# Layer 1's residual: scaled and shifted on VectorE in layer 0, loaded in pieces behind the weights

## The chip, the cores and the metric

The kernel runs on one core of one Trainium2 chip. The metric is the device time of one execution in microseconds (us). A core has TensorE (PE: matmuls and transposes), VectorE (DVE), ScalarE (ACT), GpSimd (POOL) and SyncE (SP, which here only issues loads and stores). Each engine runs its instructions in the order in which they were put, and waits on semaphores for the others.

## What is computed

Two layers of a decoder trunk on 256 tokens of width 2048, in fp32. Layer 0 is a gated linear recurrence (HGRN2), layer 1 a sparse attention (NSA). Each ends alike, with an out projection and a layer norm of the sum with its own input:

```python
def _layer_norm(x, g, b):
    mu = jnp.mean(x, -1, keepdims=True)
    xc = x - mu
    var = jnp.mean(xc * xc, -1, keepdims=True)
    return xc * lax.rsqrt(var + LN_EPS) * g + b

h = x
for i in range(2):
    y = _hgrn2_mixer(h, ...) if i == 0 else _nsa_mixer(h, ...)   # both end in (gate * o) @ w_out
    h = _layer_norm(DEEPNORM_ALPHA * h + y, ln_g[i], ln_b[i])
```

So layer 0's normed output h is needed twice in layer 1: as the input of its projections, transposed, and at the end of the layer as the residual, token by token.

## The kernel before

**Tiles.** Tokens are two tiles `t` of 128 (NT = 2). A weights tile is 256 rows by 512 columns, 512 KB: SyncE loads it as `wr` (`load`, L105), ScalarE rounds it to `wh`, and VectorE computes `wl` = `wr` - `wh` (`split`, L78 and L79), with AHEAD as their priority. A product is three matmuls: high times high, high times low, low times high (L140 to L142 in `tok_step`). A tile of weights is thus twelve matmuls of 512 columns for both token tiles. Activations are pairs of the same kind: `ah`, `al` for layer inputs (`hT.put`), `bh`, `bl` for what goes into an out projection. There are 3 slots for `wr`, 5 for `wh` and 5 for `wl`, with 1, 3 and 3 more while the pool "wide" is open (`widen`, `slot`).

**Out projection of layer 0** (L504 to L533). Four groups of 512 columns, `c` = 0 to 3, eight weights tiles each. For c < 3 both token tiles go together (`project`), and `residual` adds alpha times `xr`, a piece of x that GpSimd's queue loads (L508), into `hb` and takes statistics (L511, L512). For c = 3 the token tiles go one after the other (`project_by_tile`): `finish(t)` takes the last residual, mean and variance (L496, L497, then a power on GpSimd, L224), normalises `hb` in place (L519, four pieces), has TensorE transpose it (L196, sixteen), ScalarE scale and shift it by the norm's gain and bias (L524), which are per partition there, and splits it into `ah` and `al`. Then `hb`, normalised but neither scaled nor shifted, is stored to DRAM as `norm0` (L527, GpSimd's queue), token tile by token tile.

**Seam to layer 1.** The first projection of layer 1 (the keys, KC) runs by token tile as well. `issue_after` puts its steps for tile 0 from the eighth on (HOLD = 7) behind the last transposes of layer 0; the first seven may run ahead of them. The last transpose is what `finish` returns.

**Layer 1's out projection** (L827 on). The same four groups. `fetch(c)`, called behind the fourth weights tile, loads a piece of `norm0` (`xr`) and pieces of layer 0's gain and bias into `gb`, on SyncE's queue (L808, L811; `gb` has one buffer), and GpSimd scales and shifts `xr` (L813, L814), two passes for each token tile. `residual` adds it to the projection into `hb` (L837) and takes statistics (L839). `row` loads layer 1's own gain and bias, 1 MB each (L819), after group 1, where `widen` opens the extra slots too.

**What sets the order.** The tile framework schedules every engine from a simulated timeline and priorities. The pieces of the engines' orders further down show what came out of it for the changed places.

Of the kernel before, what the change touches and what calls it, by code (L numbers as in the profile page):

```python
# [8 lines left out]
F32 = mybir.dt.float32  # L9
# [3 lines left out]
OP = mybir.AluOpType  # L13
# [4 lines left out]
D = 2048  # L18
S = 256
NT = S // 128  # L20
KT = D // 128
KG = KT // 4
DEPTH = 2
ALPHA = (2 * DEPTH) ** 0.25
# [30 lines left out]
def trunk(ctx, tc, a, out):  # L55
    nc = tc.nc
    pe, act, dve, pool = nc.tensor, nc.scalar, nc.vector, nc.gpsimd
# [7 lines left out]
    pj = ctx.enter_context(tc.tile_pool(name="pj", bufs=4, space=PSUM))  # L65
    mx = ctx.enter_context(tc.tile_pool(name="mx", bufs=4, space=PSUM))
    dram = ctx.enter_context(tc.tile_pool(name="dram", bufs=1, space=DRAM))
    norm0 = dram.tile([S, D], F32, name="norm0")

    def pjb(shape):  # L70
        return pj.tile(shape, F32, name="pjb", tag="pjb")
# [127 lines left out]
    last = [None]  # L199
# [113 lines left out]
    with tc.tile_pool(name="start", bufs=4) as start:  # L313
# [3 lines left out]
        ps = mxb([128, 128])  # L317
# [182 lines left out]

    hT = Pair("a")
    with tc.tile_pool(name="n0", bufs=2) as n0:
        hb = n0.tile([128, NT, D], F32, name="hb", bufs=1)
        stats = n0.tile([128, NT, 4, 6], F32, name="stats", bufs=1)  # L504
        for c in range(4):
            cs = slice(512 * c, 512 * (c + 1))
            xr = n0.tile([128, NT, 512], F32, name="xr")
            nc.gpsimd.dma_start(xr, x[:, cs].rearrange("(t p) d -> p t d", p=128))  # L508

            def residual(t, ps, c=c, cs=cs, xr=xr):  # L510
                dve.scalar_tensor_tensor(hb[:, t, cs], xr[:, t], ALPHA, ps, op0=OP.mult, op1=OP.add)  # L511
                dve.bn_stats(stats[:, t, c], hb[:, t, cs])  # L512

            def finish(t, ps):
                residual(t, ps)
                mv = moments(n0, hb, stats, t)
                for g in range(KG):
                    h = hb[:, t, 512 * g:512 * (g + 1)]
                    dve.tensor_scalar(h, h, mv[:, 0:1], mv[:, 3:4], op0=OP.subtract, op1=OP.mult)  # L519
                    ps = transposed(h.rearrange("p (k d) -> p k d", d=128))  # L520
                    h1 = n0.tile([128, 4, 128], F32, name="h1")
                    for k in range(4):
                        n = 4 * g + k
                        act.activation(h1[:, k], ps[:, k], AF.Identity, scale=g0c[:, n:n + 1],  # L524
                                       bias=b0c[:, n:n + 1])
                    hT.put(g, t, h1)
                nc.gpsimd.dma_start(norm0[128 * t:128 * (t + 1), :], hb[:, t])  # L527
                return last[0]

            if c < 3:  # L530
                for t, ps in enumerate(project(oT, a["l0_w_out"], 512 * c)):
                    residual(t, ps)
            else:  # L533
                normed = project_by_tile(oT, a["l0_w_out"], 512 * c, finish)
# [96 lines left out]
    with tc.tile_pool(name="cmp", bufs=1) as cp:  # L631
# [29 lines left out]
        h = ck.hidden()  # L661
        ps = mxb([128, 4, NB])
# [8 lines left out]
        h = cv.hidden()  # L671
# [5 lines left out]
        ps = mxb([128, 4, 128])  # L677
# [4 lines left out]
        ps = ps.rearrange("p g d -> p (g d)")  # L682
# [9 lines left out]
        n = (512 + 48) // 2  # L692
# [109 lines left out]
    stats = n1.tile([128, NT, 8, 6], F32, name="stats", bufs=1)  # L802


    def fetch(c):
        cs = slice(512 * c, 512 * (c + 1))
        xr = n1.tile([128, NT, 512], F32, name="xr")
        nc.sync.dma_start(xr, norm0[:, cs].rearrange("(t p) d -> p t d", p=128))  # L808
        gb = n1.tile([128, 2, 512], F32, name="gb", bufs=1)
        for i, name in enumerate(("l0_ln_g", "l0_ln_b")):  # L810
            nc.sync.dma_start(gb[:, i], a[name][None, cs].to_broadcast([128, 512]))  # L811
        for t in range(NT):
            pool.tensor_tensor(xr[:, t], xr[:, t], gb[:, 0], op=OP.mult)  # L813
            pool.tensor_tensor(xr[:, t], xr[:, t], gb[:, 1], op=OP.add)  # L814
        return xr

    def row(name):
        r = n1.tile([128, D], F32, name=name, bufs=1)
        nc.sync.dma_start(r, a[name][None, :].to_broadcast([128, D]))  # L819
        return r  # L820


    for c in range(4):
        cs = slice(512 * c, 512 * (c + 1))

        xr = []

        def behind(j, c=c, xr=xr):
            if j == 3:
                xr.append(fetch(c))  # L830

        def residual(t, ps, c=c, xr=xr, parts=range(2)):
            xr = xr[0]
            n = ps.shape[1] // len(parts)
            for i, u in enumerate(parts):
                h = hb[:, t, 512 * c + 256 * u:512 * c + 256 * (u + 1)]
                dve.scalar_tensor_tensor(h, xr[:, t, 256 * u:256 * (u + 1)], ALPHA, ps[:, n * i:n * (i + 1)],  # L837
                                         op0=OP.mult, op1=OP.add)
                dve.bn_stats(stats[:, t, 2 * c + u], h)  # L839

        def finish(t, ps):
# [20 lines left out]
        if c < 3:  # L862
            for t, ps in enumerate(project(oT, a["l1_w_out"], 512 * c, behind)):
                residual(t, ps)
            if c == 2:
                last_xr = fetch(3)
            if c == 1:
                widen()
                g1, b1 = row("l1_ln_g"), row("l1_ln_b")
        else:  # L870
            xr.append(last_xr)
            project_by_tile(oT, a["l1_w_out"], 512 * c, finish, halve=True)
    wide.close()

# [32 lines left out]
```

## Time and profile before

| | us |
|---|---|
| median of three runs | 1019.64 |
| the runs | 1019.52, 1019.64, 1021.37 |
| the profiled execution | 1021.53 |
| its span | 1019.8 |
| TensorE busy | 999.9 (98%) |
| VectorE busy | 669.6 (66%) |
| ScalarE busy | 543.3 (53%) |
| GpSimd busy | 143.1 (14%) |
| mean granted clock of TensorE | 0.994 |

The profile is of one execution. Its rows give start and duration in us from the span's start, the engine, the line, output and input tile, and in brackets the idle time of that engine just before, with what ended it. Matmuls of 512 columns show durations of 0.39 to 0.40 but overlap: one starts every 0.2335 us, and a distance above that between two starts is time lost. The other engines' instructions overlap at their ends too, so that steps between starts are shorter than durations.

### The profile page before, as it was taken

The numbers are of one execution on the slowest core, as the hardware profiler recorded it, in microseconds if no ns is written. First come the engines' busy times: TensorE is split into PE (matmuls) and PEld (weight loads), VectorE is DVE, ScalarE is ACT, GpSimd is POOL, SyncE is SP. The second block draws the span as 40 slices with busy tenths as digits, with TensorE's granted clock in tenths as the row PEclk, the third lists the DMA queues.
The fourth block names the chain that finished last, engine by engine and source line by source line (L and its number), as shares of the span: only waits on it lengthen the run. The fifth ranks groups of instructions, "written<-read, shape, count | busy, mean of one in ns | idle before, by whom it ended". The sixth has DMA issues, their size and how long they took to land.

```text
span 1019.8 us, 15942 instructions
## 1 busy us (share of the span) xinstructions
PE 999.9 (98%) x6041; PEld 883.4 (87%) x6041; DVE 669.6 (66%) x1095; ACT 543.3 (53%) x864; POOL 143.1 (14%) x222
## 2 busy tenths in 40 slices
PE   9999999999999999999999989999999999999995
PEld 8988998899889988878889878898989889998775
DVE  6796568656866586656565655555857668675566
ACT  6654455445544554434475554454856667775241
POOL 0400300030003000210015410101010022000543
PEclk9999999999999999999999999999999999999998
DMA  8865565555555655557465677577354454345872
GB/s 299 258 218 165 155 184 168 166 155 179 173 166 155 177 176 163 161 180 250 160 208 159 200 226 238 154 222 207 106 166 143 145 165 133 119 144 184 316 240 83
DMA packets 100780, 185.25 MB, mean 182 GB/s; under 512 B 6096, under 2 KB 20512, under 8 KB 100192
## 3 DMA queue, kind: packets, MB, share of 16 engines
q1 hardware_dynamic: 99232, 178.67, 56.7%
q0 software_dynamic: 1472, 5.56, 1.7%
q8 instruction: 47, 0.77, 0.3%
q14 instruction: 29, 0.24, 0.1%
HBM read 180.02 MB, written 4.19 MB: 181 GB/s over the span
## 4 chain that ended last, share of the span: by engine, by line
PE 84%; DMA 7%; DVE 3%; POOL 2%; ACT 2%; issue 1%; SPq 0%; ACTq 0%; DVEq 0%; POOLq 0%
PE pjb L141 15%; PE pjb L142 15%; PE pjb L140 15%; PE pjb L185 10%; PE pjb L187 10%; PE pjb L188 10%; DMA wr<-in_l_w_in_dram 3%; PE mxb L423 2%; DVE wl L79 2%; DMA wr<-in_l_w_out_dram 2%; ACT wh L78 1%; DMA gb<-in_l_ln_g_dram 1%; PE mxb L196 1%; POOL fl L590 1%; PE mxb L546 1%; PE mxb L548 1%
## 5 line engine op out<-in xcount | busy, mean ns | idle before, releaser
L79 DVE TENSOR_TENSOR wl<-wr,wh 128x1024 fp32r<-128x1024 f32 (+2 forms) x330 | 398.9, 1213 | 224.2 <-ACT wh L78 221.5
L78 ACT ACTIVATE wh<-wr 128x1024 fp32r<-128x1024 f32 (+2 forms) x330 | 340.7, 1036 | 346.1 <-PE pjb L142 149.9
L185 PE MATMUL pjb<-ah,wh 128*128 128x256 f32 x832 | 235.8, 284 | 0.5 <-ACT wh L78 0.5
L187 PE MATMUL pjb<-al,wh 128*128 128x256 f32 x832 | 235.9, 284 | 0.0
L188 PE MATMUL pjb<-ah,wl 128*128 128x256 f32 x832 | 234.4, 284 | 0.5 <-DVE wl L79 0.5
L141 PE MATMUL pjb<-wl,ah 128*128 128x512 f32 (+1 forms) x576 | 223.6, 388 | 2.2 <-DVE wl L79 2.1
L142 PE MATMUL pjb<-wh,al 128*128 128x512 f32 (+1 forms) x576 | 222.7, 387 | 0.0
L140 PE MATMUL pjb<-wh,ah 128*128 128x512 f32 (+1 forms) x576 | 221.4, 387 | 1.1 <-ACT wh L78 1.1
L185 PEld LDWEIGHTS pjb<-ah,wh 128*128 128x128 f32 x832 | 157.3, 189 | 1.5 <-ACT wh L78 1.0
L188 PEld LDWEIGHTS pjb<-ah,wl 128*128 128x128 f32 x832 | 156.6, 189 | 1.1 <-DVE wl L79 0.9
L187 PEld LDWEIGHTS pjb<-al,wh 128*128 128x128 f32 x832 | 156.5, 188 | 0.5
L141 PEld LDWEIGHTS pjb<-wl,ah 128*128 128x128 f32 x576 | 108.8, 189 | 26.0 <-DVE wl L79 4.4
L140 PEld LDWEIGHTS pjb<-wh,ah 128*128 128x128 f32 x576 | 108.5, 189 | 23.6 <-ACT wh L78 1.8
L142 PEld LDWEIGHTS pjb<-wh,al 128*128 128x128 f32 x576 | 108.9, 189 | 22.2
L141 PE MATMUL pjb<-wl,bh 128*128 128x512 f32 (+1 forms) x272 | 105.0, 386 | 1.4 <-DVE wl L79 1.3
L142 PE MATMUL pjb<-wh,bl 128*128 128x512 f32 (+1 forms) x272 | 104.1, 384 | 0.0
L140 PE MATMUL pjb<-wh,bh 128*128 128x512 f32 (+1 forms) x272 | 103.1, 384 | 0.8 <-ACT wh L78 0.8
L141 PEld LDWEIGHTS pjb<-wl,bh 128*128 128x128 f32 x272 | 51.2, 188 | 13.9 <-DVE wl L79 3.2
L140 PEld LDWEIGHTS pjb<-wh,bh 128*128 128x128 f32 x272 | 51.1, 188 | 12.3 <-ACT wh L78 1.7
L142 PEld LDWEIGHTS pjb<-wh,bl 128*128 128x128 f32 x272 | 51.3, 189 | 10.4
L486 POOL TENSOR_TENSOR gz<-gz,gn 128x512 f32<-128x512 f32 x8 | 13.5, 1691 | 317.0 <-ACT gz L485 316.4
L557 POOL TENSOR_TENSOR rot<-qr,cc 128x128 f32<-128x128 f32 x14 | 9.5, 678 | 254.1 <-ACT qr L553 253.8
(220 smaller groups left out, 1034.0 us busy)
## 6 DMA issues: line engine op xcount, KB each, us to landing
wr<-in_l_w_in_dram SPq DMA_DIRECT2D x230, 512.0 KB, 3.7
wr<-in_l_w_out_dram SPq DMA_DIRECT2D x64, 512.0 KB, 4.4
wr<-in_l_w_in_dram SPq DMA_DIRECT2D x16, 280.0 KB, 3.0
wr<-in_l_cmp_w_k_dram SPq DMA_DIRECT2D x8, 512.0 KB, 4.4
wr<-in_l_cmp_w_v_dram SPq DMA_DIRECT2D x8, 512.0 KB, 4.3
xr<-in_x_dram POOLq DMA_DIRECT2D x4, 512.0 KB, 5.7
norm<-hb POOLq DMA_DIRECT2D x2, 1024.0 KB, 5.4
xr<-norm SPq DMA_DIRECT2D x4, 512.0 KB, 7.2
```

What stands on the lines that cost most here:

```text
L78: act.activation(hi, src, AF.Copy)
L79: dve.tensor_tensor(lo, src, hi.bitcast(F32), op=OP.subtract)
L140: pe.matmul(ps, xh, wh, start=(k == 0), stop=False)
L141: pe.matmul(ps, xh, wl, start=False, stop=False)
L142: pe.matmul(ps, xl, wh, start=False, stop=(k == KT - 1))
L185: pe.matmul(o, hi[:, kk, c], xh, start=(k == 0 and b % 2 == 0), stop=False, skip_group_check=True)
L187: pe.matmul(o, hi[:, kk, c], xl, start=False, stop=False, skip_group_check=True)
L188: pe.matmul(o, lo[:, kk, c], xh, start=False, stop=(k == KT - 1), skip_group_check=True)
L196: last[0] = pe.transpose(ps[:, i], src[:, i], ident).ins
L423: pe.matmul(ps[:, h], km[:, h].rearrange("p b r j -> p (b r j)"), later, start=True, stop=True)
L486: pool.tensor_tensor(z, z, gn, op=OP.mult)
L546: pe.matmul(o, a[0], b[0], start=start, stop=False)
```

## The change

Layer 0's gain and bias are loaded whole, as rows repeated over 128 partitions, by two loads of 1 MB on GpSimd's queue ahead of layer 0's residual. After the transposes of each token tile, VectorE multiplies and adds them into `hb` in place (16 passes of 128x512 in all), and the result is stored as `res1`. In layer 1 the passes on GpSimd and `fetch` are gone: `res1` is loaded into `hb` itself in four pieces, layer 1's gain and bias in eight pieces, and each call of `behind` puts one of these twelve loads behind a weights tile. `widen` is called after group 0.

```diff
+        rows = []
+        for name in ("l0_ln_g", "l0_ln_b"):
+            r = n0.tile([128, D], F32, name=name, bufs=1)
+            nc.gpsimd.dma_start(r, a[name][None, :].to_broadcast([128, D]))
+            rows.append(r)
         hb = n0.tile([128, NT, D], F32, name="hb", bufs=1)
...
                     hT.put(g, t, h1)
-                nc.gpsimd.dma_start(norm0[128 * t:128 * (t + 1), :], hb[:, t])
-                return last[0]
+                done = last[0]
+                for g in range(KG):
+                    cs = slice(512 * g, 512 * (g + 1))
+                    for r, op in zip(rows, (OP.mult, OP.add)):
+                        dve.tensor_tensor(hb[:, t, cs], hb[:, t, cs], r[:, cs], op=op)
+                nc.gpsimd.dma_start(res1[128 * t:128 * (t + 1), :], hb[:, t])
+                return done
...
-    def fetch(c):
-        cs = slice(512 * c, 512 * (c + 1))
-        xr = n1.tile([128, NT, 512], F32, name="xr")
-        nc.sync.dma_start(xr, norm0[:, cs].rearrange("(t p) d -> p t d", p=128))
-        gb = n1.tile([128, 2, 512], F32, name="gb", bufs=1)
-        for i, name in enumerate(("l0_ln_g", "l0_ln_b")):
-            nc.sync.dma_start(gb[:, i], a[name][None, cs].to_broadcast([128, 512]))
-        for t in range(NT):
-            pool.tensor_tensor(xr[:, t], xr[:, t], gb[:, 0], op=OP.mult)
-            pool.tensor_tensor(xr[:, t], xr[:, t], gb[:, 1], op=OP.add)
-        return xr
...
+    g1, b1 = (n1.tile([128, D], F32, name=name, bufs=1) for name in ("l1_ln_g", "l1_ln_b"))
+    loads = []
+    for c in range(4):
+        cs = slice(512 * c, 512 * (c + 1))
+        loads.append((hb[:, :, cs], res1[:, cs].rearrange("(t p) d -> p t d", p=128)))
     for c in range(4):
         cs = slice(512 * c, 512 * (c + 1))
+        for r, name in ((g1, "l1_ln_g"), (b1, "l1_ln_b")):
+            loads.append((r[:, cs], a[name][None, cs].to_broadcast([128, 512])))
+
+    def behind(j):
+        if loads and j > 0:
+            nc.sync.dma_start(*loads.pop(0))
...
-                dve.scalar_tensor_tensor(h, xr[:, t, 256 * u:256 * (u + 1)], ALPHA, ps[:, n * i:n * (i + 1)],
-                                         op0=OP.mult, op1=OP.add)
+                dve.scalar_tensor_tensor(h, h, ALPHA, ps[:, n * i:n * (i + 1)], op0=OP.mult, op1=OP.add)
...
-            if c == 2:
-                last_xr = fetch(3)
-            if c == 1:
+            if c == 0:
                 widen()
-                g1, b1 = row("l1_ln_g"), row("l1_ln_b")
```

VectorE at the seam, before: from the first `wl` behind tile 0's normalising to tile 1's normalising (L519). L511 is tile 1's residual.

```order
L79 TENSOR_TENSOR wl<-wr,wh 128x1024 x2
L79 TENSOR_TENSOR al<-h_4848,ah 128x4x128
L79 TENSOR_TENSOR wl<-wr,wh 128x1024
L79 TENSOR_TENSOR al<-h_4861,ah 128x4x128
L79 TENSOR_TENSOR wl<-wr,wh 128x1024
L511 SCALAR_TENSOR_TENSOR hb<-xr,pjb 128x512
L512 BN_STATS stats<-hb 128x6
L496 BN_AGGR mv<-stats 128x2
L497 TENSOR_SCALAR mv<-mv 128x1
L79 TENSOR_TENSOR wl<-wr,wh 128x1024
L519 TENSOR_SCALAR hb<-hb,mv 128x512 x4
```

After, the same stretch, with one `wl` ahead of its first row. L537 are the new passes on `hb`, and L516 is tile 1's residual:

```order
L537 TENSOR_TENSOR hb<-hb,l_ln_g 128x512
L79 TENSOR_TENSOR wl<-wr,wh 128x1024
L537 TENSOR_TENSOR hb<-hb,l_ln_g 128x512 x3
L537 TENSOR_TENSOR hb<-hb,l_ln_b 128x512
L79 TENSOR_TENSOR al<-h_4852,ah 128x4x128
L537 TENSOR_TENSOR hb<-hb,l_ln_b 128x512
L79 TENSOR_TENSOR wl<-wr,wh 128x1024
L537 TENSOR_TENSOR hb<-hb,l_ln_b 128x512
L79 TENSOR_TENSOR al<-h_4865,ah 128x4x128
L537 TENSOR_TENSOR hb<-hb,l_ln_b 128x512
L79 TENSOR_TENSOR wl<-wr,wh 128x1024 x2
L516 SCALAR_TENSOR_TENSOR hb<-xr,pjb 128x512
```

Between the residual of tile 1 and its normalising (L524) stand now:

```order
L79 TENSOR_TENSOR wl<-wr,wh 128x1024
L79 TENSOR_TENSOR al<-h_4878,ah 128x4x128
L79 TENSOR_TENSOR wl<-wr,wh 128x1024
L79 TENSOR_TENSOR al<-h_4891,ah 128x4x128
L517 BN_STATS stats<-hb 128x6
L496 BN_AGGR mv<-stats 128x2
L497 TENSOR_SCALAR mv<-mv 128x1
L524 TENSOR_SCALAR hb<-hb,mv 128x512 x4
```

Eight passes and one `wl` have come between tile 0's normalising and tile 1's residual, and two `wl` and two `al` between that residual and its statistics. TensorE's order at this place is the same in both kernels.

SyncE at layer 1's out projection, before (L105 are the weights, L808 and L811 the loads of `fetch`, L819 the rows):

```order
L105 DMA wr<-in_l_w_out_dram 128x2x512 x15
L808 DMA xr<-norm_72 128x2x512
L811 DMA gb<-in_l_ln_g_dram 128x512
L811 DMA gb<-in_l_ln_b_dram 128x512
L808 DMA xr<-norm_72 128x2x512
L819 DMA l_ln_g<-in_l_ln_g_dram 128x2048
L819 DMA l_ln_b<-in_l_ln_b_dram 128x2048
L105 DMA wr<-in_l_w_out_dram 128x2x512 x3
L811 DMA gb<-in_l_ln_g_dram 128x512
L811 DMA gb<-in_l_ln_b_dram 128x512
L808 DMA xr<-norm_72 128x2x512
L105 DMA wr<-in_l_w_out_dram 128x2x512 x3
```

After (L829 are the twelve pieces):

```order
L105 DMA wr<-in_l_w_out_dram 128x2x512 x16
L829 DMA hb<-res_72 128x2x512 x4
L829 DMA l_ln_g<-in_l_ln_g_dram 128x512
L829 DMA l_ln_b<-in_l_ln_b_dram 128x512
L829 DMA l_ln_g<-in_l_ln_g_dram 128x512
L829 DMA l_ln_b<-in_l_ln_b_dram 128x512
L829 DMA l_ln_g<-in_l_ln_g_dram 128x512
L829 DMA l_ln_b<-in_l_ln_b_dram 128x512
L829 DMA l_ln_g<-in_l_ln_g_dram 128x512
L829 DMA l_ln_b<-in_l_ln_b_dram 128x512
L105 DMA wr<-in_l_w_out_dram 128x2x512 x16
```

The twelve pieces stand in one block behind the sixteenth weights tile, where before loads of `fetch` and of weights alternate.

ScalarE at the last gate of layer 1, before: `o` is the last head group's output, `zT` its gate, `bh` what goes into the out projection.

```order
L78 ACTIVATE pt_8778<-mxb 128x512
L78 ACTIVATE wh<-wr 128x1024 x2
L774 ACTIVATE o<-mxb 128x512
L786 ACT_TABLE_LOAD
L786 ACTIVATE zT<-pjb 128x512
L78 ACTIVATE bh<-o 128x4x128 x2
```

After:

```order
L78 ACTIVATE pt_8798<-mxb 128x512
L78 ACTIVATE wh<-wr 128x1024 x2
L785 ACTIVATE o<-mxb 128x512
L78 ACTIVATE wh<-wr 128x1024
L797 ACT_TABLE_LOAD
L797 ACTIVATE zT<-pjb 128x512
```

One `wh` of the out projection has moved from behind `bh` to a place between `o` and the table load for the gate.

## Rows read from the trace of the kernel before

**Rows 1.** Page, parts 1, 4, 5: busy time and share; chain that ended last; ScalarE's `wh`.

```profile
PE 999.9 (98%) x6041; PEld 883.4 (87%) x6041; DVE 669.6 (66%) x1095; ACT 543.3 (53%) x864; POOL 143.1 (14%) x222
...
PE 84%; DMA 7%; DVE 3%; POOL 2%; ACT 2%; issue 1%; SPq 0%; ACTq 0%; DVEq 0%; POOLq 0%
...
L78 ACT ACTIVATE wh<-wr 128x1024 fp32r<-128x1024 f32 (+2 forms) x330 | 340.7, 1036 | 346.1 <-PE pjb L142 149.9
```

**Rows 2.** Timeline of VectorE at the seam: start, duration, line, tile, [idle before].

```profile
502.02 2.35 DVE L79 TENSOR_TENSOR wl<-wr,wh 128x1024 fp32r<-128x1024 f32 x2
...
507.51 0.69 DVE L79 TENSOR_TENSOR al<-h,ah 128x512 fp32r<-128x512 f32 x1
...
508.12 1.22 DVE L79 TENSOR_TENSOR wl<-wr,wh 128x1024 fp32r<-128x1024 f32 x1
...
509.55 0.69 DVE L511 SCALAR_TENSOR_TENSOR hb<-xr,pjb 128x512 f32<-128x512 f32 x1 [0.22 <-PE pjb L142]
...
511.30 0.15 DVE L497 TENSOR_SCALAR mv<-mv 128x1 f32<-128x1 f32 x1
...
512.73 1.91 DVE L519 TENSOR_SCALAR hb<-hb,mv 128x512 f32<-128x512 f32 x4
```

**Rows 3.** Timelines of TensorE and ScalarE at the seam.

```profile
514.27 1.91 PE L196 MATMUL mxb<-ident,hb 128*128 128x128 f32 x16
...
527.73 0.58 ACT L553 ACTIVATE qr<-pjb 128x512 f32<-128x512 f32 x1
```

**Rows 4.** Windows: length, busy us of PE, PEld, DVE, ACT, POOL, clock, DMA share, GB/s.

```profile
598.00:599.00 1.00, 0.04 (x1) 0.04 (x1) 0.10 (x2) 0.91 (x1) 0.00 (x0) 1.00 0.42 146
601.00:602.00 1.00, 1.00 (x3) 0.78 (x3) 1.00 (x2) 0.47 (x2) 0.60 (x2) 0.50 0.54 134
600.00:610.00 10.00, 9.78 (x48) 8.32 (x49) 5.84 (x7) 6.26 (x11) 1.54 (x4) 0.83 0.78 245
```

**Rows 5.** Timelines of GpSimd, VectorE and TensorE in layer 0's out projection.

```profile
448.95 1.47 POOL L508 DMA_DIRECT2D xr<-in_x_dram  x2 [6.48 <-PE mxb L231]
...
454.69 1.28 DVE L511 SCALAR_TENSOR_TENSOR hb<-xr,pjb 128x512 f32<-128x512 f32 x2 [1.97 <-DMA xr<-in_x_dram]
...
462.62 0.40 PE L140 MATMUL pjb<-wh,bh 128*128 128x512 f32 x1
```

**Rows 6.** DMA issues: queue, count, size of one, median us from issue to landing.

```profile
xr<-in_x_dram POOLq DMA_DIRECT2D x4, 512.0 KB, 5.7
...
norm<-hb POOLq DMA_DIRECT2D x2, 1024.0 KB, 5.4
...
l_ln_b<-in_l_ln_b_dram SPq DMA_DIRECT2D x1, 1024.0 KB, 11.7
```

**Rows 7.** TensorE in layer 1's out projection: timeline at two places, one window.

```profile
953.39 0.40 PE L142 MATMUL pjb<-wh,bl 128*128 128x512 f32 x1
...
955.55 0.40 PE L142 MATMUL pjb<-wh,bl 128*128 128x512 f32 x1
...
990.50 0.40 PE L140 MATMUL pjb<-wh,bh 128*128 128x512 f32 x1
...
995.19 0.39 PE L142 MATMUL pjb<-wh,bl 128*128 128x512 f32 x1
...
950.00:960.00 10.00, 9.32 (x40) 6.89 (x38) 4.53 (x3) 3.57 (x4) 3.80 (x3) 1.00 1.02 378
```

**Rows 8.** Timelines of SyncE (first `xr`) and TensorE (its last matmul).

```profile
937.31 0.37 SPq L808 DMA_DIRECT2D xr<-norm  x1
...
1008.21 0.28 PE L142 MATMUL pjb<-wh,bl 128*128 128x256 f32 x1
```

**Rows 9.** Timelines of ScalarE and TensorE at the last gate of layer 1.

```profile
932.90 1.28 ACT L786 ACT_TABLE_LOAD   x1
...
934.19 0.60 ACT L786 ACTIVATE zT<-pjb 128x512 f32<-128x512 f32 x1
...
935.35 0.40 PE L140 MATMUL pjb<-wh,bh 128*128 128x512 f32 x1
```

More of the change, by code (lines that the diff above doesn't have):

```diff
@@ L67, in trunk @@
     dram = ctx.enter_context(tc.tile_pool(name="dram", bufs=1, space=DRAM))
-    norm0 = dram.tile([S, D], F32, name="norm0")
+    res1 = dram.tile([S, D], F32, name="res1")
     def pjb(shape):
@@ L802, in trunk, with residual @@
     stats = n1.tile([128, NT, 8, 6], F32, name="stats", bufs=1)
-    def fetch(c):
-        cs = slice(512 * c, 512 * (c + 1))
-        xr = n1.tile([128, NT, 512], F32, name="xr")
-        nc.sync.dma_start(xr, norm0[:, cs].rearrange("(t p) d -> p t d", p=128))
-        gb = n1.tile([128, 2, 512], F32, name="gb", bufs=1)
-        for i, name in enumerate(("l0_ln_g", "l0_ln_b")):
-            nc.sync.dma_start(gb[:, i], a[name][None, cs].to_broadcast([128, 512]))
-        for t in range(NT):
-            pool.tensor_tensor(xr[:, t], xr[:, t], gb[:, 0], op=OP.mult)
-            pool.tensor_tensor(xr[:, t], xr[:, t], gb[:, 1], op=OP.add)
-        return xr
[L817 to L820, printed above, removed]
+    g1, b1 = (n1.tile([128, D], F32, name=name, bufs=1) for name in ("l1_ln_g", "l1_ln_b"))
+    loads = []
     for c in range(4):
         cs = slice(512 * c, 512 * (c + 1))
[L826 to L833, printed above, removed]
+        loads.append((hb[:, :, cs], res1[:, cs].rearrange("(t p) d -> p t d", p=128)))
[6 more added lines that the diff above has]
+            nc.sync.dma_start(*loads.pop(0))
+    for c in range(4):
+        cs = slice(512 * c, 512 * (c + 1))
+        def residual(t, ps, c=c, parts=range(2)):
             n = ps.shape[1] // len(parts)
@@ L864, in trunk @@
                 residual(t, ps)
-            if c == 2:
-                last_xr = fetch(3)
-            if c == 1:
+            if c == 0:
                 widen()
-                g1, b1 = row("l1_ln_g"), row("l1_ln_b")
         else:
-            xr.append(last_xr)
             project_by_tile(oT, a["l1_w_out"], 512 * c, finish, halve=True)
```

## The prediction

> **What bounds the kernel now.** I read the shares first: TensorE is busy 98% of the span and the chain that ended last is 84% TensorE [rows 1]. So a step costs or gives time only where TensorE then waits, and the question for each edit is whether TensorE's own order reaches an instruction before its input is there. Next I read the timelines of VectorE and TensorE at the seam of layer 0 and layer 1 [rows 2, 3], because the change puts new work on VectorE there. Then the table of short windows for what a pause of TensorE does to its clock [rows 4], the start of layer 0's out projection [rows 5, 6], and the out projection of layer 1, where rows and weights share the loads [rows 7, 8, 9]. The span of the profiled execution is 1019.8 us inside a run of 1021.53; the median of the runs is 1019.64. My sum is a difference, made from the profiled rows and added to the median.
>
> **Part 1: sixteen VectorE passes at the seam.** Layer 0's last column group goes token tile by token tile. After tile 0 the changed order holds eight scale or shift passes (L537) between tile 0's normalising and tile 1's residual (the order of VectorE above). In before that stretch runs from 502.02 to 509.55 with four `wl`, two `al` and about 1.5 us of waiting [rows 2]. Two `wl` in a row took 2.35 us, the second of them 1.22 as always, so a `wl` steps by 1.13; an `al` of 128x512 steps by 0.61 (507.51 to 508.12). No row shows an in-place `hb` pass; the nearest is that `al`, also a two-input fp32 pass of 128x512 in SBUF, and the four normalising passes of the same size with one tensor input are a lower bound (from 1.91 us for four). I take 0.61.
>
> The new stretch has five `wl`, two `al` and eight passes: 5 x 1.13 + 10 x 0.61 = 11.75 us, so tile 1's residual starts at 502.02 + 11.75 = 513.8 instead of 509.55. VectorE is in order, so everything behind it is late too. Behind that residual the new order has two `wl` and two `al` ahead of the statistics, which before had one `wl`, beside GpSimd's power: 2 x 1.13 + 2 x 0.61 = 3.5 us. The residual, its statistics and the two small steps are 1.75 us from L511 to L497 [rows 2], and from L497 to a first scaled tile some 0.9 us more (0.25 for L497 and 0.6 for the power on GpSimd). So tile 1's normalising starts at 513.8 + 3.5 + 1.75 + 0.9 = 519.9, where before it started at 512.73. Its first pass takes 0.5, and the transposes can begin at 520.4.
>
> TensorE reached those transposes at 514.27 without waiting [rows 3]. Its order is the same in the changed kernel: all it may do ahead of them is tile 0's first seven steps of the next projection, and these end at 514.27. **It waits 520.4 - 514.27 = 6.1 us.** The bounds are 5.0 (passes at 0.48) and 7.0 (passes at their full 0.69). Tile 1's own eight passes stand behind its normalising, off the path. All later work hangs on TensorE, so nothing absorbs the loss. The stores of the scaled tiles are late too: tile 1's leaves GpSimd's queue behind its passes, at 519.9 + 1.9 + 8 x 0.61 + 2 x 0.61 = 527.9; with the landing of before, 5.4 [rows 3, 6], that is 533.3. The rotary copies that take over the space come at 527.73 [rows 3] behind TensorE's next tile, so with the pause and the clock at 535.5 or later: no cost, 1 us at most if the passes run late.
>
> **The clock after that pause.** In before TensorE was busy for 0.04 of the microsecond from 598; from 601 the granted clock read 0.50 (1.2 GHz), and 0.83 over 600 to 610, with 1.00 before and after [rows 4]. That is 10 x 0.17 = 1.7 us of matmul time lost after a pause of little over 1 us. A pause of 6 us should cost as much: **+1.7**, with 1.0 and 3.3 (twice the row, for a longer pause) as bounds.
>
> **Part 2: two whole rows loaded ahead of layer 0's residual.** Each is 1 MB, on GpSimd's queue, and the first `xr` (0.52 MB) stands behind them. In before that `xr` was issued at 448.95 and the first residual began at 454.69 [rows 5]. TensorE needs that residual's PSUM bank back for the third column group, whose first matmul is at 462.62 [rows 5], by counting back from 514.27. Now 2.62 MB go ahead of it. At the best rate of a row, 378 GB/s [rows 7], that is 6.9 us; the plain `xr` of before took 5.7 to land [rows 6], of which 1.4 is its bytes at this rate, so 4.3 are latency and sharing: 448.95 + 6.9 + 4.3 = 460.2, in time. If the weights keep half the rate, 13.9 + 4.3 gives 467.1, and with 0.7 for the residual TensorE waits 5.2 us. The second whole-row load of layer 1 landed 11.7 us after its issue with 2.5 MB queued ahead of its own [rows 6], some 300 GB/s, nearer to the fast end. I take **+1.0**, bounds 0 and 5.2. The split weights have 5 + 3 slots here, tiles of twelve matmuls, 2.8 us each, so they are ahead by enough to cover a VectorE that stands still for 10 us.
>
> The Trainium skill, page "DMA: Bandwidth & Descriptors", section "Queues, rings and completion order", says that each DMA engine takes turns between the queues that have work, a packet at a time. By that rule the slow end would hold whenever weights are queued, and the sum would be 4 us longer; no row here shows the shares of two busy queues, so it is a rival below.
>
> **Part 3: layer 1's out projection loses its fetches.** In before, eight multiplies and eight adds on GpSimd prepare `xr`; the loads of `gb` wait in SyncE's queue for these, with weights behind them. TensorE pays in two places. From 953.39 to 955.55 it took 2.16 us for four steps of 0.2335, a loss of 1.23. From 990.50 to 995.19 it took 4.69 us for eight such steps and six halves, a loss of 2.1 [rows 7]. Together 3.35 us.
>
> In the changed order SyncE issues sixteen weights tiles, then the twelve pieces, then sixteen weights (the order above). No piece waits for GpSimd, and 4 MB of rows are loaded in place of 6 MB. The wait for the last `bl` at the head of the pieces stays, as `xr` had it. The pieces start where the first `xr` load stood, 937.31; 4.2 million bytes at 378 GB/s take 11 us, and with 4.3 of latency and 1.4 of its own bytes the seventeenth tile lands by 954, split by 957. TensorE ends at 1008.2 [rows 8], and the last sixteen tiles are 45 us of it, or 48 with the loss at 990: it is wanted at about 960. So I expect **-3.35** (bounds -3.35 and 0; the tile is in time by 3 us, so I take the full gain).
>
> **Part 4: the extra slots open one group earlier.** A sixteenth tile is loaded before the pieces, and its `wh` now stands on ScalarE between the last `o` and the table load for `zT` (the order of ScalarE above). In before the table load ran at 932.90 and `zT` at 934.19, ended 934.79 [rows 9]. A `wh` takes 1.04 in the mean [rows 1], and more if its tile lands after 932.9: `zT` ends at 935.8 to 936.9. TensorE needs the bank that `zT` reads for the first matmul of group one's token tile 1, at 935.35 [rows 9]. **It waits 0.5 to 1.5; I take +1.1.** The tail behind TensorE's end keeps its order: 0.
>
> **Sum.** 6.1 + 1.7 + 1.0 - 3.35 + 1.1 = +6.55 us. Against the profiled run that is 1028.1, against the median **1026.2 us**.
>
> **Rivals.**
> - *The passes fall into VectorE's idle time.* VectorE was idle a third of the span [rows 1], and 1.5 us at the seam. If the passes cost TensorE nothing, parts 3 and 4 remain: -3.35 + 1.1 = -2.25, 1017.4, faster. It decides when the delay of tile 1's normalising stays under 1 us: its first result was there at 513.2 and was wanted at 514.27. Against it: 4.8 us of passes and three more `al` or `wl` stand in an in-order queue ahead of it. Chance 0.08.
> - *The pieces don't do what they say.* They are not behind single loads any more but in one block of 4 MB, and the tile after them may be late as before. Then none of the 3.35 us comes back: 1019.64 + 9.9 = 1029.5. For it: from 950 to 960 the DMA engines were full, share 1.02 [rows 7]. Against it: the sixteen tiles in front. Chance 0.12.
> - *The whole rows hold up layer 0's first residual*, the slow end of part 2: 4.2 more, and a clock drop of its own of up to 1.7: 1030.4 to 1032.1. Chance 0.10.
> - *The clock is not lowered at the seam.* 1026.2 - 1.7 = 1024.5. Against it the rows at 601. Chance 0.08.
> - *Half price*: passes at 0.48 us and the last `wl` and `al` where TensorE is not waiting, say 3 us, clock 1.0, rows hidden: 3.0 + 1.0 - 2.25 = +1.75, 1021.4, no change. Chance 0.07.
>
> **How the numbers follow.** The forecast has 0.55. Its own terms reach from 1023 (5.0 + 1.0 + 0 - 3.35 + 0.5 = +3.15) to some 1029 with two of them half way to their upper bounds. Leaving out the first rival and half of the slow ends, the range is 1021.3 to 1030. 0.2% is 2 us, about what a measurement of this kernel can tell from no change. Faster: the first rival, 0.08. Same: half price and some of the low end, 0.09. Slower: the rest, 0.83.
>
> **What would show it.** Right: in VectorE's timeline eight passes between tile 0's normalising and tile 1's residual, and tile 1's normalising at about 520; a pause of 5 to 7 us on TensorE in front of the second sixteen transposes, waiting for VectorE; a granted clock of 0.50 for some microseconds behind it; no pauses at 950 to 995 (shifted by 7 to 9 us), and one of about 1 us at the first group for tile 1, waiting for ScalarE's `zT`. Wrong: a pause under 3 us at the seam, or weights that land late behind the pieces; a pause near 463 that waits for VectorE's first residual would mean the slow end of part 2.

## The result and the profile after

The changed kernel takes 1026.04 us in the median of four runs (1024.85 to 1026.49) against 1020.3 of before beside it; the ratio is 1.0051 with an interval of 1.0036 to 1.0066. It is slower by some 5.7 us, where 1026.2 was forecast. The profiled execution of after took 1025.88 (span 1024.2).

The page of after, busy time and the chain, answers to [rows 1]:

```profile
PE 998.6 (98%) x6041; PEld 883.4 (86%) x6041; DVE 677.1 (66%) x1111; ACT 543.2 (53%) x864; POOL 120.9 (12%) x208
...
PE 86%; DMA 5%; DVE 4%; ACT 2%; POOL 1%; issue 1%; SPq 0%; ACTq 0%; DVEq 0%; POOLq 0%
```

TensorE is busy for 1.3 us less than before and the span is 4.4 longer, so it waits 5.7 us more. The list of what TensorE waited for, the three lines that before doesn't have (us in total, times, longest):

```profile
PE mxb L196 <- DVE hb L524: 5.8, 1, 5.8
...
PE pjb L140 <- DVE hb L516: 0.6, 1, 0.6
...
PE pjb L140 <- ACT zT L797: 0.6, 1, 0.6
```

By far the longest is the one of 5.8 us: the transposes wait for the normalising of tile 1. VectorE's timeline at the seam, against [rows 2], and TensorE's, against [rows 3]:

```profile
505.64 1.89 DVE L537 TENSOR_TENSOR hb<-hb,l_ln_g 128x512 f32<-128x512 f32 x3
...
514.46 0.69 DVE L516 SCALAR_TENSOR_TENSOR hb<-xr,pjb 128x512 f32<-128x512 f32 x1
...
520.41 1.92 DVE L524 TENSOR_SCALAR hb<-hb,mv 128x512 f32<-128x512 f32 x4 [0.70 <-POOL mv L224]
```

```profile
514.77 0.40 PE L142 MATMUL pjb<-wh,al 128*128 128x512 f32 x1
...
521.01 3.44 PE L196 MATMUL mxb<-ident,hb 128*128 128x128 f32 x16 [5.84 <-DVE hb L524]
...
524.20 0.48 PE L140 MATMUL pjb<-wh,ah 128*128 128x512 f32 x1
```

In before the next matmul behind the sixteen transposes of 514.27 was this one:

```profile
515.94 0.48 PE L140 MATMUL pjb<-wh,ah 128*128 128x512 f32 x1
```

The passes L537 stand between tile 0 and the residual of tile 1, which starts at 514.46 (509.55 in before); the normalising follows at 520.41 (512.73). TensorE's last matmul ahead of the transposes starts at 514.77 and takes its step of 0.2335, so the transposes are 521.01 - 515.00 = 6.0 us late. From the end of tile 0's normalising to the start of tile 1's, VectorE took 17.65 us against 10.71 in before. The eight passes are 4.8 of the difference, and two `wl` and two `al` that came forward in the order are 3.5; some 1.5 us in which VectorE had been idle took up the rest. Behind the wait the sixteen transposes need 3.19 us to the next matmul, against 1.67 in before (514.27 to 515.94). The windows there (columns as in [rows 4]) show why:

```profile
518.00:520.00 2.00, 0.00 (x0) 0.00 (x0) 1.64 (x5) 0.00 (x0) 0.20 (x1) 0.50 1.05 407
...
522.00:524.00 2.00, 2.00 (x11) 2.00 (x10) 1.97 (x4) 1.84 (x6) 0.00 (x0) 0.50 0.03 8
...
524.00:526.00 2.00, 2.00 (x12) 1.68 (x11) 2.00 (x5) 2.00 (x6) 0.00 (x0) 0.98 0.00 0
```

The granted clock falls in the pause itself, is 0.50 to 524, and 0.98 in the window after that: 3.19 - 1.67 = 1.5 us.

The first residual of layer 0, timelines of GpSimd, VectorE and TensorE, against [rows 5]:

```profile
448.80 0.56 POOL L506 DMA_DIRECT2D l_ln_g<-in_l_ln_g_dram  x1 [6.46 <-PE mxb L231]
...
462.51 1.29 DVE L516 SCALAR_TENSOR_TENSOR hb<-xr,pjb 128x512 f32<-128x512 f32 x2 [3.13 <-DMA xr<-in_x_dram]
...
462.25 0.40 PE L142 MATMUL pjb<-wh,bl 128*128 128x512 f32 x1
...
463.25 0.50 PE L140 MATMUL pjb<-wh,bh 128*128 128x512 f32 x1 [0.60 <-DVE hb L516]
```

`xr` is there at 462.5 and not at 454.7; TensorE loses 1.00 - 0.2335 = 0.77 before the third column group and 0.1 behind it. Layer 1, timelines of SyncE, ScalarE and TensorE, against [rows 7 to 9]:

```profile
946.58 1.90 SPq L829 DMA_DIRECT2D hb<-res  x4
...
956.19 12.22 SPq L105 DMA_DIRECT2D wr<-in_l_w_out_dram  x6
...
941.09 1.06 ACT L78 ACTIVATE wh<-wr 128x1024 fp32r<-128x1024 f32 x1 [0.19 <-DMA wr<-in_l_w_out_dram]
...
942.16 1.28 ACT L797 ACT_TABLE_LOAD   x1
...
943.46 0.60 ACT L797 ACTIVATE zT<-pjb 128x512 f32<-128x512 f32 x1
...
964.27 1.06 ACT L78 ACTIVATE wh<-wr 128x1024 fp32r<-128x1024 f32 x1 [14.59 <-DMA wr<-in_l_w_out_dram]
...
943.14 0.39 PE L142 MATMUL pjb<-wh,bl 128*128 128x512 f32 x1
...
944.11 0.50 PE L140 MATMUL pjb<-wh,bh 128*128 128x512 f32 x1 [0.58 <-ACT zT L797]
```

The pieces stand in a block from 946.58, the next weights tile is issued at 956.19, and its `wh` runs at 964.27. No matmul of TensorE waits for it: from 950 to the end of the projection there is no step with a loss over 0.15, where before has six, 3.3 us in all, and 3.9 with the 0.1 that most of them leave in the step or two behind. The `wh` at 941.09 stands ahead of the table load, and `zT` is 1.2 us late against its place in before; TensorE loses 0.74 and 0.1.

### The profile page after: what moved, and what is told of

Its sections match the earlier page's. It is cut to its first block, busy times and chain, and to the rows that moved or that the text cites. A ratio compares the mean times of both kernels' runs of the same rounds, so it can differ in the third digit from the quotient of the medians.

```text
span 1024.2 us, 15939 instructions
## 1 busy us (share of the span) xinstructions
PE 998.6 (98%) x6041; PEld 883.4 (86%) x6041; DVE 677.1 (66%) x1111; ACT 543.2 (53%) x864; POOL 120.9 (12%) x208
## 4 chain that ended last, share of the span: by engine, by line
PE 86%; DMA 5%; DVE 4%; ACT 2%; POOL 1%; issue 1%; SPq 0%; ACTq 0%; DVEq 0%; POOLq 0%
PE pjb L140 16%; PE pjb L142 15%; PE pjb L141 15%; PE pjb L187 10%; PE pjb L188 10%; PE pjb L185 10%; DMA wr<-in_l_w_in_dram 3%; DVE wl L79 2%; PE mxb L423 2%; ACT wh L78 1%; PE mxb L196 1%; DMA xr<-in_x_dram 1%; POOL fl L601 1%; PE mxb L557 1%; PE mxb L559 1%; PE mxb L558 1%
```

## The experiments

Their ratios are against runs of the kernel before on the same chip (its medians there: 1020.76, 1020.99 and 1020.55). Waits are read as losses: the distance between the starts of two matmuls, less TensorE's step (0.2335 us for 512 columns, half of it for 256). Line numbers shift by a few between the kernels; the tiles' names don't.

**Parts 3 and 4 alone.**

```diff
-        rows = []
-        for name in ("l0_ln_g", "l0_ln_b"):
-            r = n0.tile([128, D], F32, name=name, bufs=1)
-            nc.gpsimd.dma_start(r, a[name][None, :].to_broadcast([128, D]))
-            rows.append(r)
...
-                for g in range(KG):
-                    cs = slice(512 * g, 512 * (g + 1))
-                    for r, op in zip(rows, (OP.mult, OP.add)):
-                        dve.tensor_tensor(hb[:, t, cs], hb[:, t, cs], r[:, cs], op=op)
```

> The changed kernel without the sixteen passes on VectorE and without the two whole-row loads in layer 0 (parts 3 and 4 alone); the residual of layer 1 is thus left unscaled and unshifted. Theory: the loss sits at the seam. TensorE's wait of 6.0 us before tile 1's transposes, the slow clock behind it (1.5) and the wait for the first residual (0.9) all go: 1026.0 - 8.4 = 1017.6, faster than before by about 2.7, with the one wait of 0.8 for zT left and none behind the pieces. Rival: the loss sits in layer 1, where pieces and slots were moved; then the time stays above 1023.

Measured: 1017.32, ratio 0.9973 (0.9962 to 0.9985). No wait at the seam or at 462, no wait for weights in layer 1, and one wait of TensorE for `zT` (0.84 in steps):

```profile
PE pjb L140 <- ACT zT L788: 0.7, 1, 0.7
```

So the loss of the changed kernel is in layer 0. Its layer 1 gains 2.8 us by the ratio (1.5 to 3.9), where the traces' losses give 3.9 less 0.9. The rival falls.

**Parts 1 and 2 alone.** Layer 0 of after, layer 1 of before, which loads what layer 0 stored (against before, layer 1's part):

```diff
-        nc.sync.dma_start(xr, norm0[:, cs].rearrange("(t p) d -> p t d", p=128))
+        nc.sync.dma_start(xr, res1[:, cs].rearrange("(t p) d -> p t d", p=128))
```

> Layer 0 of the changed kernel (whole rows loaded, sixteen passes on VectorE, the scaled residual stored) with layer 1 of the kernel before, which scales and shifts it once more on GpSimd; the residual is thus scaled twice. Theory: parts 1 and 2 cost 6.0 (wait) + 1.5 (clock) + 0.9 (first residual) wherever layer 1 stands: 1020.8 + 8.4 = 1029.2, and the waits for weights in layer 1's out projection are back, some 3.4 us in all. Rival: a part of the seam's loss is made up later, since the weights run ahead during the pause: under 1027.5.

Measured: 1029.49, ratio 1.0083 (1.0068 to 1.0098), 8.5 us. TensorE's timeline and a window:

```profile
464.00 0.50 PE L140 MATMUL pjb<-wh,bh 128*128 128x512 f32 x1 [1.15 <-DVE hb L516]
...
521.74 3.67 PE L196 MATMUL mxb<-ident,hb 128*128 128x128 f32 x16 [5.84 <-DVE hb L524]
```

```profile
526.00:528.00 2.00, 2.00 (x6) 1.51 (x5) 2.00 (x5) 0.82 (x2) 0.00 (x0) 0.56 0.00 0
```

The wait at the seam is 5.84 idle, 6.0 in steps, as in after; at 464 it is 1.3 and not 0.8, and the waits for weights in layer 1 are back, eight of them, 3.7 us. Nothing of the loss is made up later. The clock stays low here to 527.8 (0.56 in the window), so that the transposes and the six matmuls behind them lose 2.9 us and not 1.5. The profiled execution is the slowest of its four, 1031.76: its terms add up to more than the 8.5 of the ratio.

**The passes behind tile 1.** `scaled` holds the last normalising instruction of VectorE:

```diff
                 normed = project_by_tile(oT, a["l0_w_out"], 512 * c, finish)
+                with tc.issue_after(scaled[0]):
+                    for t in range(NT):
+                        for g in range(KG):
+                            cs = slice(512 * g, 512 * (g + 1))
+                            for r, op in zip(rows, (OP.mult, OP.add)):
+                                dve.tensor_tensor(hb[:, t, cs], hb[:, t, cs], r[:, cs], op=op)
+                        nc.gpsimd.dma_start(res1[128 * t:128 * (t + 1), :], hb[:, t])
```

> The changed kernel with the same sixteen passes, put on VectorE behind tile 1's normalising for both token tiles. Theory: it is the place in VectorE's order that costs, not the work. The order now has only two wl and one al too many between tile 1's residual and its last normalised piece, so TensorE waits some 2 us in two pieces instead of 6.0; with the clock lowered less or not at all: 1020 to 1022.5. Rival: VectorE's extra 10 us cost where ever they stand, because it is near its limit there: above 1024.5.

Measured: 1021.49, ratio 1.0010 (1.0001 to 1.0019). VectorE's first passes and TensorE's transposes:

```profile
516.88 2.49 DVE L547 TENSOR_TENSOR hb<-hb,l_ln_g 128x512 f32<-128x512 f32 x4
...
514.52 1.63 PE L196 MATMUL mxb<-ident,hb 128*128 128x128 f32 x12 [0.62 <-DVE hb L525]
...
517.11 0.63 PE L196 MATMUL mxb<-ident,hb 128*128 128x128 f32 x4 [0.96 <-DVE hb L525]
```

The first of the sixteen passes starts at 516.88, behind the normalising, and TensorE loses 0.78 in front of its transposes and 1.3 among them instead of 6.0. The clock is not lowered. So it is the place in VectorE's order that costs. It isn't a better kernel: two `wl` and an `al` more than in before still come between tile 1's residual and its last normalised piece.

**The pause filled**, to separate the clock from the wait. Dummy matmuls, 48 and then 24 of them, follow tile 1's last out projection step (`last_mm`), so that the seven steps of the next projection move into the pause:

```diff
                 residual(t, ps)
+                if t == 1:
+                    with tc.issue_after(last_mm[0]):
+                        fill = mxb([128, 128])
+                        for _ in range(FILL):
+                            pe.matmul(fill, ident, ident, start=True, stop=True)
```

> The changed kernel with 48 dummy matmuls of 128x128 put on TensorE behind tile 1's last out projection step, some 5.0 us, where it would wait for VectorE anyway. Theory: the sixteen transposes took 3.2 us instead of 1.7 because the granted clock fell in the pause. With the pause filled the clock reads 1.00 at the seam, the transposes take 1.7 to 2.2, and the time falls by about 1.5 to 1024.5. Rival: the transposes are slow because the normalised pieces arrive one by one; then they take 3.2 us at a full clock too, and the time stays at 1026 or goes up.

Measured: 1029.5, ratio 1.0086 (1.0073 to 1.0099). The filling was mis-sized: 48, which the rows count as 96, took 10.64 us (509.75 to 520.39), more than the pause. TensorE's timeline and a window:

```profile
509.75 10.88 PE L528 MATMUL mxb<-ident 128*128 128x128 f32 x96
...
525.39 1.91 PE L199 MATMUL mxb<-ident,hb 128*128 128x128 f32 x16
```

```profile
524.00:526.00 2.00, 2.00 (x13) 1.68 (x12) 0.00 (x0) 0.00 (x0) 0.00 (x0) 1.00 0.00 0
```

The clock reads 1.00 throughout, and the sixteen take 1.91 (3.44 in after). This alone doesn't rule out the rival: they start at 525.39, when all four pieces had been normalised for 3 us (VectorE's four took from 520.07 to 521.99). With half the size the transposes again follow VectorE piece by piece:

> The changed kernel with 24 dummy matmuls in place of 48; 48 took 10.6 us, so these take 5.3, inside the pause of 6. Theory: the pause is filled without a loss, the clock stays at 1.00, the sixteen transposes take 1.7 to 1.9 instead of 3.2, and the time falls by 1.5 to 1024.5 to 1025. Rival: the pause is only moved and the transposes are slow all the same: 1026 to 1027.

```profile
509.44 5.52 PE L528 MATMUL mxb<-ident 128*128 128x128 f32 x48
...
520.37 2.09 PE L199 MATMUL mxb<-ident,hb 128*128 128x128 f32 x16 [0.49 <-DVE hb L532]
```

```profile
520.00:522.00 2.00, 1.63 (x14) 1.46 (x15) 2.00 (x5) 0.94 (x3) 0.00 (x0) 1.00 0.26 95
```

Measured: 1025.13, ratio 1.0049 (1.0033 to 1.0064). The 24 ran from 509.44 to 514.72, the clock stays at 1.00 at the seam, and the transposes reach the next matmul in 1.84 us, though VectorE began the first piece only at 519.77. So they were slow in after through the clock. TensorE still loses 0.65 ahead of them. The clock's part is shown by these rows alone: in the time, 0.9 us less than after in the medians and 0.2 by the ratios, it is lost in the intervals.

**Rows behind the second `xr`.**

```diff
             nc.gpsimd.dma_start(xr, x[:, cs].rearrange("(t p) d -> p t d", p=128))
+            if c == 1:
+                for name in ("l0_ln_g", "l0_ln_b"):
+                    r = n0.tile([128, D], F32, name=name, bufs=1)
+                    nc.gpsimd.dma_start(r, a[name][None, :].to_broadcast([128, D]))
+                    rows.append(r)
```

> The changed kernel with the two whole-row loads behind the second xr load on GpSimd's queue. Theory: the first residual doesn't wait for 2 MB any more, TensorE has no wait at about 462 (it was 0.8 to 0.9): 1026.0 - 0.9 = 1025.1. Rival: the wait is for weights or for VectorE's order and stays.

Measured: 1024.9, ratio 1.0046 (1.0032 to 1.0059). There is no loss at 462 in its trace, and VectorE's first residual is back at its place in before:

```profile
454.80 1.29 DVE L517 SCALAR_TENSOR_TENSOR hb<-xr,pjb 128x512 f32<-128x512 f32 x2 [2.09 <-DMA xr<-in_x_dram]
```

But with the rows in front this residual starts at the very edge of what TensorE can bear, and the wait differs between executions: 0.77 in after, 1.31 with parts 1 and 2 alone, 0.54 with 48 dummies, 0.1 with 24, and none with the passes behind tile 1 or with the slots behind group 1. In these six traces the residual starts at 460.59 to 463.26. So the place of the rows moves the residual by 6 to 8 us, but the 1.1 us in the medians can't be put down to it.

**Slots behind group 1 again.**

```diff
-            if c == 0:
+            if c == 1:
                 widen()
```

> The changed kernel with the extra slots opened behind group 1 again, as in before. Theory: ScalarE's wh no longer stands ahead of the gate's table load, so TensorE's wait of 0.8 us at group one's first matmul for token tile 1 goes: 1026.0 - 0.8 = 1025.2, if the tiles behind the block of pieces still come in time. Rival: the earlier slots are what bridges the pieces; without the sixteenth tile in front of them TensorE waits 1 to 3 us for weights at about 960: 1026.2 to 1028.2.

Measured: 1026.75, ratio 1.0063 (1.0050 to 1.0076). The wait for `zT` is gone, and this has come:

```profile
961.04 0.40 PE L142 MATMUL pjb<-wh,bl 128*128 128x512 f32 x1
...
962.67 0.72 PE L140 MATMUL pjb<-wh,bh 128*128 128x512 f32 x2 [1.23 <-ACT wh L78]
...
963.93 0.50 PE L141 MATMUL pjb<-wl,bh 128*128 128x512 f32 x1 [0.54 <-DVE wl L79]
```

From 961.04 to 963.93 there are three steps, so 2.2 us are lost, for `wh` of the first weights behind the pieces. The rival holds: without the sixteenth tile in front the block of pieces is felt. By the traces part 4 costs 0.8 and saves 2.2; in the time the two kernels' intervals overlap.

**The early slots in the kernel before.**

```diff
-            if c == 1:
+            if c == 0:
                 widen()
+            if c == 1:
                 g1, b1 = row("l1_ln_g"), row("l1_ln_b")
```

> The kernel before with the extra slots opened behind group 0: part 4 alone. Theory: TensorE gets the wait of 0.8 us for zT, the early slots bridge the first wait for weights (1.2 us), and the waits that come from SyncE behind gb's one buffer (0.4 and 2.1) stay: 1020.9 + 0.8 - 1.2 = 1020.5. Rival: the slots bridge all the waits for weights: 1018.

Measured: 1020.4, ratio 0.9998 (0.9990 to 1.0007), no difference. Its trace, with a span of 1017.4, shows one wait for `zT` of 1.05 in steps and only 0.7 for weights in the projection. By the one trace, of one of the faster executions, the rival is right; by twelve runs nothing is gained, as the theory had it (1020.5). Why the other executions don't show the gain stays open.

**The passes left on GpSimd, pieces in tiles of their own.** Layer 0 as before; in layer 1 `hb` is loaded directly and scaled in place:

```diff
+    gb = n1.tile([128, 2, D], F32, name="gb", bufs=1)
...
+                for t in range(NT):
+                    for i, op in enumerate((OP.mult, OP.add)):
+                        pool.tensor_tensor(hb[:, t, cs], hb[:, t, cs], gb[:, i, cs], op=op)
```

> Layer 0 as in the kernel before (no passes on VectorE), layer 1 with loads in pieces straight into hb, layer 0's gain and bias in pieces of their own tiles (no buffer to wait for), and the sixteen passes in place on GpSimd as in before; extra slots behind group 0. Theory: what held the weights in before was SyncE's wait for GpSimd and the one buffer of gb, so the gain of 3.4 to 3.8 comes without VectorE's passes: 1020.3 - 3.6 + 0.8 = 1017.5. Rival: it was the 6 MB of rows themselves, which are as many here as before: 1020 to 1021.

Measured: 1021.91, ratio 1.0018 (1.0007 to 1.0028). The time is the rival's, 0.9 above the end of its range; the windows behind the pieces, columns as in [rows 4]:

```profile
950.00:960.00 10.00, 9.35 (x41) 7.21 (x39) 0.07 (x1) 1.06 (x1) 9.62 (x9) 1.00 1.02 344
...
960.00:970.00 10.00, 8.73 (x36) 6.57 (x36) 8.88 (x11) 3.13 (x4) 5.28 (x3) 1.00 0.95 341
```

The DMA share is 1.02 and 0.95, TensorE busy 9.35 and 8.73 of ten: 2.9 us are lost for weights. That it is the amount of rows doesn't follow from this, since GpSimd's passes stand beside them. Moving layer 1's own gain and bias behind the fifth tile of the last group leaves 4 MB ahead (`during(j)` loads them at j = 4, in four loads behind that tile's):

```diff
-        ws = [weights(w, j, c0, 512) for j in range(KT // 2)]
+        ws = []
+        for j in range(KT // 2):
+            ws.append(weights(w, j, c0, 512))
+            if during:
+                during(j)
```

> As the kernel with the passes on GpSimd in layer 1 and pieces in tiles of their own, but layer 1's own gain and bias (2 MB) are loaded behind the fifth weights tile of the last group, so only 4 MB stand ahead of and between the weights of groups 2 and 3. Theory: what was late there were weights behind 6 MB of rows; with 4 MB TensorE has only its wait for zT: 1020.8 - 3.4 + 0.8 = 1018.2. Rival: GpSimd's passes hold VectorE's wl, or the pieces stand in the way as a block in any size: 1020 to 1022.

Measured: 1022.93, ratio 1.0021 (1.0010 to 1.0031). Again nearer the rival, 0.9 above its range. SyncE's first piece, ScalarE's first `wh` behind the pieces, and one window, here and then in the kernel with parts 3 and 4 alone, which loads as many bytes there:

```profile
938.03 0.37 SPq L834 DMA_DIRECT2D hb<-res  x1
...
959.15 1.06 ACT L79 ACTIVATE wh<-wr 128x1024 fp32r<-128x1024 f32 x1 [17.91 <-DMA wr<-in_l_w_out_dram]
...
940.00:950.00 10.00, 10.00 (x45) 8.02 (x44) 5.79 (x11) 1.24 (x2) 6.72 (x6) 1.00 0.89 265
```

```profile
937.91 1.90 SPq L820 DMA_DIRECT2D hb<-res  x4
...
955.17 1.06 ACT L78 ACTIVATE wh<-wr 128x1024 fp32r<-128x1024 f32 x1 [14.16 <-DMA wr<-in_l_w_out_dram]
...
940.00:950.00 10.00, 10.00 (x44) 8.07 (x43) 5.36 (x11) 1.01 (x1) 0.00 (x0) 1.00 0.99 344
```

From the first piece to that `wh` it is 21.1 us here and 17.3 there, at 265 against 344 GB/s in the same ten us; TensorE then loses 1.5 at 959 here and nothing there. Later it loses 2.3 more for weights at 990, where the norm's rows now stand ahead of the last ones, and 1.5 at the clock of 0.50 that follows. Why the same bytes go slower is open: the order of the loads (a residual piece and two row pieces in turn) and GpSimd's work beside them differ, and no run took these apart. Beside that work three `wl` took 5.75 us from 960.24 on, where three took 3.49 in before (468.15). With the slots behind group 1:

> The same with the extra slots behind group 1. Theory: without the wait for zT 1017.4. Rival: the early slots bridge the pieces; then TensorE waits 1 to 3 us for the first weights behind them and the time is 1018.4 to 1020.4.

Measured: 1027.13, ratio 1.0059 (1.0047 to 1.0072), worse than either expectation:

```profile
959.61 1.22 PE L144 MATMUL pjb<-wh,bh 128*128 128x512 f32 x2 [5.55 <-ACT wh L79]
```

The first weights behind the pieces are 5.7 us late, and more follows at half the clock. It agrees with the slots run above in sign: without the early slots the pieces are felt.

**Two buffers for `gb` in the kernel before, and early slots.**

```diff
-        gb = n1.tile([128, 2, 512], F32, name="gb", bufs=1)
+        gb = n1.tile([128, 2, 512], F32, name="gb", bufs=2)
...
-            if c == 1:
+            if c == 0:
                 widen()
+            if c == 1:
                 g1, b1 = row("l1_ln_g"), row("l1_ln_b")
```

> The kernel before with the extra slots behind group 0 and two buffers for gb, so that SyncE doesn't wait for GpSimd at the head of the loads: no part of the residual is moved to layer 0. Theory: the waits for weights are those of a queue that stands still, so they go: 1020.9 - 3.8 + 0.8 = 1017.9. Rival: they come from 6 MB of rows in a row, as with the pieces of their own tiles: 1020 to 1022.

Measured: 1018.76, ratio 0.9984 (0.9975 to 0.9992), faster than both kernels, though by 1.6 us where the theory had 3.0. SyncE at the loads of layer 1, and two windows:

```profile
943.68 0.96 SPq L105 DMA_DIRECT2D wr<-in_l_w_out_dram  x1
...
946.37 2.60 SPq L105 DMA_DIRECT2D wr<-in_l_w_out_dram  x3
```

```profile
945.00:955.00 10.00, 10.00 (x45) 8.03 (x44) 3.76 (x9) 1.06 (x1) 9.94 (x8) 1.00 1.00 334
...
955.00:965.00 10.00, 10.00 (x44) 8.07 (x43) 5.66 (x10) 2.12 (x2) 0.10 (x1) 1.00 1.04 376
```

Weights stand between the rows again (943.68, 946.37), the DMA engines are as full as anywhere (1.00 and 1.04), and TensorE loses 0.95 for `zT` and 0.15 for weights instead of 3.3. So 6 MB of rows can be loaded with hardly a wait if weights go between them. What the second buffer adds is seen in the medians only: 1018.76 against 1020.40 with the early slots alone. In the traces the early slots alone had already left no more than 0.7 of the waits for weights, so that these rows don't show that SyncE's wait at the head of its queue was what held them.

## Why the prediction was right, step by step

- **Passes at the seam**: 6.1 forecast, 6.0 measured, in after, in parts 1 and 2 alone and in the two runs with rows or slots moved. The order gave the number of instructions, the `al` row gave the price: three passes in a row took 1.89 (the row at 505.64), with 0.69 for the last one a step of 0.60, against the 0.61 that was taken. Residual and normalising of tile 1 stand at 514.46 and 520.41, where 513.8 and 519.9 were forecast; part 2 has delayed both engines by 0.7 there. In the first rival "three more `al` or `wl`" is a miscount: by the orders it is four.
- **Clock**: 1.7 forecast, 1.5 in after's trace. That it came so near is luck of this execution: in the traces of three kernels with the same pause (slots behind group 1, rows behind the second `xr`, parts 1 and 2 alone) the clock is back later after the pause and the loss is 2.5, 2.8 and 2.9, inside the bounds of 1.0 to 3.3. The run with 24 dummies shows that it is the clock.
- **Whole rows**: 1.0 forecast, 0.9 measured, but between 0 and 1.4 from execution to execution. The 1.0 was picked between bounds of 0 and 5.2 and not worked out, so that the hit is luck; that the fast end was nearer was read rightly from [rows 6]. `xr` came 8 us later than in before: 13.7 us from the first issue to the residual, less the 4.3 of latency and sharing, is 2.62 MB in 9.4 us, 279 GB/s, between the 378 of the fast end and half of that. The trace's packets show why the slow end didn't come. From 451 to 455 GpSimd's queue had the DMA engines to itself. From 456 to 460 both queues were at work, with 243 packets of GpSimd's and 241 of SyncE's; but GpSimd's packets are of 4 and 8 KB and the weights' of 2 KB, so that it was 1.11 MB against 0.47. The Trainium skill's page "DMA: Bandwidth & Descriptors", section "Queues, rings and completion order", has the engines take turns a packet at a time; the trace agrees. The step from equal turns to half the rate, in the prediction, was wrong here.
- **Fetches gone**: -3.35 forecast from two places; all the waits for weights in this projection were 3.9, and they are gone. The reason was only half of it. The forecast put the gain down to the wait for GpSimd at the head of the queue, and no run shows that by itself: the run with two buffers for `gb` has the early slots too. In the changed kernel the early slots carry a good part, since without them 2.2 us come back. I had part 4 down as a cost only. The first tile behind the pieces was split at 966.6 and wanted at 968.1, in time by 1.5 us where 3 were forecast.
- **Early slots**: 1.1 forecast for `zT`, 0.8 measured.
- **Sum**: 6.0 + 1.5 + 0.9 - 3.9 + 0.8 = 5.3; the medians differ by 5.7, and the ratio gives 5.2. The two profiled executions differ by 4.35 only: the slowed clock at 600 in before's [rows 4] isn't in after's trace, where TensorE's losses from 570 to 650 are 0.3 smaller, the tail behind its last matmul is 0.4 shorter, and the rest is spread over small steps. That the forecast of 6.55 came within 1 us of the medians is in part luck, since the clock and the rows vary by more than 1 us each between executions.
- **Rivals**: that the passes fall into idle time is out by the 5.8 us wait; that the pieces leave the weights late holds for the kernels without early slots or with GpSimd's passes, not for this one. A single trace can't tell more than some 1 us here: the medians' intervals reach 1 to 1.5 us to either side.

## What to carry to other kernels

An engine's idle share says nothing on where new work may go: ten us of passes on an engine that is idle a third of the time cost 6 us, because eight of them, and four small steps that the new order brought forward with them, stood in an in-order queue ahead of the one instruction that the bound engine waited for. They cost 2 us when put behind it. Read the order of the engine at that place, count what stands ahead, and price it with the nearest row. A gain and a loss of one change are best taken apart by running each part alone: here a gain of 1.6 us was to be had with one more buffer and the early slots, without the part that cost 8.5.

## What the runs showed of the hardware

- The granted clock fell to 0.50 within a pause of 6.0 us, but not always at the same place in it. In after the window from 516 to 518 reads 0.81, so it fell 2.2 us into the pause, and was back at 1.00 3.1 us behind the pause's end. With parts 1 and 2 alone the window from 520 to 522 reads 0.74: it fell 5.2 us into the pause and was back 6.0 us behind its end. The same pause thus cost 1.5 us in the one and 2.9 in the other.
- A plain fp32 matmul of 128x128 took 0.222 us (48 in 10.64), a transpose of the same shape 0.104 (sixteen in 1.67), both at a clock of 1.00.
- Two DMA queues that were both at work sent about as many packets each, so that the queue with the larger packets moved more: 1.11 MB in 243 packets against 0.47 in 241, in after from 456 to 460, and 1.08 in 249 against 0.47 in 242 with parts 1 and 2 alone.
- A `wl` beside GpSimd's passes took 2.25 us instead of 1.21; which of the two engines loses differs. VectorE and GpSimd in the trace of before:

```profile
962.50 1.21 DVE L79 TENSOR_TENSOR wl<-wr,wh 128x1024 fp32r<-128x1024 f32 x1
...
970.92 2.25 DVE L79 TENSOR_TENSOR wl<-wr,wh 128x1024 fp32r<-128x1024 f32 x1 [2.49 <-ACT wh L78]
...
970.78 3.53 POOL L814 TENSOR_TENSOR xr<-xr,gb 128x512 f32<-128x512 f32 x2
```

The Trainium skill, page "SBUF — State Buffer", section "Who interferes with whom", says that a VectorE instruction with two inputs in SBUF and a GpSimd instruction that reads SBUF hold each other up; the row at 970.92, against 962.50 where GpSimd was idle, agrees. At 966.40 it was GpSimd that waited: one of its passes took 3.18 instead of 1.29, while two `wl` beside it took 1.21 and 1.22. It moved no term of the sum.
